# A gated activation that stays in its PSUM bank, its low part subtracted by VectorE instead of GpSimd

## The chip, the core and the metric

The kernel runs on one core of a Trainium2 chip. The core has five engines that run side by side and wait for each other through semaphores: TensorE (PE, matmuls; its weight loads are listed apart as PEld), VectorE (DVE), ScalarE (ACT), GpSimd (POOL) and SyncE (SP, which here only issues transfers). Data lies in SBUF and in PSUM, which has banks of 512 fp32 values per partition and takes the matmul results. The metric is the device time of one execution, in microseconds; lower is better.

## The reference

One decoder layer for 512 prompt tokens and 32 sample tokens: a mixer (RWKV-7 heads and windowed attention), and then PEER, a retrieval among 16384 experts. The change lies in PEER only, which is, cut down:

```python
def block(hb):                                  # hb: tokens x 1024
    q = (hb @ w_query).reshape(PEER_BLOCK, PEER_HEADS, 2, D_HALF)
    s = jnp.einsum('thcd,cnd->thcn', q, sub_keys)
    s1, i1 = lax.top_k(s[:, :, 0], PEER_TOPK)
    s2, i2 = lax.top_k(s[:, :, 1], PEER_TOPK)
    ...                                         # the best 16 of the sums, per head: idx, gate
    pre = jnp.einsum('td,tkd->tk', hb, eu[idx])
    act = jax.nn.gelu(pre, approximate=False) * gate
    return jnp.einsum('tk,tkd->td', act, ev[idx])
```

So every token picks 128 of the 16384 rows of `expert_u` and `expert_v` (eu, ev; 1024 values each).

## The kernel before

The prompt is cut into four tiles of 128 tokens. Two of them (tiles 0 and 3, and the 32 sample tokens) are done by **gathers**, the other two (1 and 2, together ND = 256 tokens) by the **dense part**, which multiplies by all 16384 experts, with gates that are zero where an expert was not picked.

*The gather side.* `experts` walks through a tile's 128 picks: GpSimd issues an indirect DMA that fetches one row of eu per token (`gat`, 128x1024, five buffers), VectorE makes a dot product of it into `pre`; after Gelu and gate, the same walk over ev, where VectorE adds `act * gat` to the sum (`x`). Each such gather with its use is a step of the queue `side`; `beside(n)` takes n steps on average.

*The dense part* runs over 128 blocks of 128 experts. All fp32 values are split into a high part (rounded to fp32r) and a low part (the rest), and products are made as high times high, low times high and high times low.
- `block_in` loads a block of eu and ev (`uv`), transposes eu through TensorE into two banks of the PSUM pool `w` (four banks in turn), copies the high part uH with ScalarE and takes the low part uL with VectorE; of ev, ScalarE makes vH and GpSimd makes vL.
- `block_u` multiplies with the tokens (24 matmuls into a bank `pre`, which the profile lists under `w`), takes Gelu in place on ScalarE, multiplies by the gates in two halves of 128 tokens on VectorE (the "gating": first half from `gl`, second from `gA` or `gB`), and splits the product into aH (ScalarE) and aL.
- `block_v` multiplies these with vH and vL into four banks `acc` (24 matmuls).

The loop calls `block_u(j+1)`, `block_in(j+2)`, `block_v(j)`, then up to two steps of `late`, which makes the projections and the top-k of tile 3 during the first blocks (the names that begin with l), and then three steps of the gather side:

```python
        for _ in range(LATE):
            next(more, None)
        with tc.issue_after(mark), tc.issue_after(sub):
            beside(RATE_D)
```

`mark` is the instruction that made aL, `sub` the last uL. The order on each engine is not the program's: the compiler's scheduler sets it when the kernel is built, from a model of its own, and `issue_after` only keeps the gather steps behind the instructions named, on the same engine.

Of the kernel before, what the change touches and what calls it, by code (L numbers as in the profile page):

```python
# [11 lines left out]
F32 = mybir.dt.float32  # L12
# [3 lines left out]
OP = mybir.AluOpType  # L16
# [97 lines left out]
def hymba_step(ctx, tc, x_prompt, x_sample, cache_k, cache_v, state_wkv, state_shift, meta, norm1_g, w_in, mu, w0,  # L114
# [3 lines left out]
    A, G, T, DM = nc.scalar, nc.gpsimd, nc.tensor, nc.sync  # L118
# [11 lines left out]
    V = V()  # L130
    uid = [0]

    def _t(pool, tag, bufs, shape, dt=F32):
        uid[0] += 1
        return pool.tile(list(shape), dt, tag=tag, name=f"{tag}_{uid[0]}", bufs=bufs)
# [1271 lines left out]
    ND = 256  # L1407
# [3 lines left out]
    def dt_(tag, bufs, shape, dt=F32):  # L1411
        return _t(dn, tag, bufs, shape, dt)

    def dps():
        return _t(dp, "w", 4, [128, 512])
# [40 lines left out]
    def block_u(x, g):  # L1456
        uH, uL, vH, vL = x
        pre = dps()[:, 0:ND]
        for k in range(8):
            T.matmul(pre, uH[:, k, :], hH[:, k, :], start=(k == 0), stop=False)  # L1460
            T.matmul(pre, uH[:, k, :], hL[:, k, :], start=False, stop=False)  # L1461
        for k in range(8):
            T.matmul(pre, uL[:, k, :], hH[:, k, :], start=False, stop=(k == 7))  # L1463
        ac = dt_("ac", 2, [128, ND])
        A.activation(pre, pre, AF.Gelu)  # L1465
        for i in range(2):
            V.tensor_tensor(ac[:, 128 * i:128 * i + 128], pre[:, 128 * i:128 * i + 128], g[i], OP.mult)
        aH = dt_("aH", 2, [128, ND], F32R)
        aL = dt_("aL", 2, [128, ND], F32R)
        A.copy(aH, ac)  # L1470
        return (vH, vL, aH, aL), G.tensor_tensor(aL, ac, aH.bitcast(F32), OP.subtract).ins  # L1471

    def block_v(j, x):
        vH, vL, aH, aL = x
# [98 lines left out]

    ins = {j: block_in(j)[0] for j in range(2)}
    mid, last = block_u(ins.pop(0), gate_of(0))
    for j in range(128):
        nxt, mark = None, last
        if j < 127:
            nxt, last = block_u(ins.pop(j + 1), gate_of(j + 1))
        if j < 126:  # L1580
            ins[j + 2], sub = block_in(j + 2)
        block_v(j, mid)
        mid = nxt
# [4 lines that stand above are left out]
# [45 lines left out]
```

## Time and profile before

| | us |
|---|---|
| median of 3 runs | 2225.62 |
| lowest and highest run | 2205.1 and 2230.73 |
| profiled execution | 2230.96 |
| its span in the trace | 2229.0 |
| busy in the span: TensorE, VectorE, GpSimd, ScalarE | 1852.5, 1712.3, 1426.3, 869.6 |

The profile is of one execution. Its busy times are shares of the whole span, which has a first part (mixer, up to about 1110 us), the making of the gate tables (to 1245 us), the dense part (to 2210 us) and an end of 19 us. Times of rows are microseconds from the start of the span. Line 126 is the helper through which every VectorE instruction is recorded, so VectorE's instructions are told apart by their tiles.

### The profile page before, as it was taken

How to read it: one execution, taken by the hardware profiler on the slowest of the kernel's cores; microseconds unless marked ns; L12 is line 12 of the kernel's file. 1: busy time of each engine (PE TensorE's matmuls, PEld its weight loads, DVE VectorE, ACT ScalarE, POOL GpSimd, SP SyncE). 2: the span in 40 equal slices, each digit the busy share in tenths (PEclk: the TensorE clock that was granted, in tenths of full speed). 3: DMA queues.
4: the chain of work that ended last, by engine and by line, in shares of the span. 5: the costliest groups of instructions: out<-in, count | busy, mean ns of one | idle time of the engine just before them, and what ended most of it. 6: DMA issues, size and time to landing. Idle time of an engine off the chain costs nothing.

```text
span 2229.0 us, 37454 instructions
## 1 busy us (share of the span) xinstructions
PE 1852.5 (83%) x13915; PEld 1720.4 (77%) x13915; DVE 1712.3 (77%) x3265; ACT 869.6 (39%) x1963; POOL 1426.3 (64%) x1091
## 2 busy tenths in 40 slices
PE   5899975585859858897366898899999999999995
PEld 5889974374737747786366888899999999999995
DVE  5543436788787888799889689987666688999897
ACT  6654421211313324223189534343444444343333
POOL 0110103878674767465615457899898999999996
PEclk9999996555655769998679999999999999999998
DMA  7532472687785798997667887799999999998886
GB/s 219 158 107 75 136 188 86 232 276 236 258 285 161 235 310 292 284 310 236 187 212 253 300 285 250 274 325 335 332 327 330 334 312 322 310 320 307 312 300 210
DMA packets 310156, 569.51 MB, mean 256 GB/s; under 512 B 32787, under 2 KB 194565, under 8 KB 309830
## 3 DMA queue, kind: packets, MB, share of 16 engines
q0 software_dynamic: 84048, 305.70, 39.7%
q1 hardware_dynamic: 225926, 261.43, 36.3%
q8 instruction: 109, 1.79, 0.3%
q14 instruction: 73, 0.60, 0.1%
HBM read 543.07 MB, written 24.60 MB: 255 GB/s over the span
## 4 chain that ended last, share of the span: by engine, by line
PE 38%; DVE 21%; issue 13%; POOL 12%; DMA 11%; ACT 4%; SPq 0%; DVEq 0%; POOLq 0%; ACTq 0%
POOL gat L1032 7%; DVE gat L126 4%; DVE x L126 4%; PE pD L218 3%; PE acc L1479 3%; PE acc L1480 3%; PE w L1463 3%; PE acc L1478 3%; PE w L1460 3%; PE w L1461 3%; DMA gat<-in_expert_u_dram,ei 2%; PE w L1446 2%; POOL aL L1471 2%; POOL vL L1453 2%; DMA gat<-in_expert_v_dram,ei 2%
## 5 line engine op out<-in xcount | busy, mean ns | idle before, releaser
L126 DVE SCALAR_TENSOR_TENSOR x<-gat,act,x 128x1024 f32<-128x1024 f32 x287 | 497.6, 1734 | 27.7 <-DMA gat<-in_expert_v_dram,ei 25.8
L1032 POOL DMA_INDIRECT gat<-in_expert_u_dram,ei x256 | 352.5, 1377 | 111.8 <-DVE pre L126 52.7
L1032 POOL DMA_INDIRECT gat<-in_expert_v_dram,ei x256 | 330.9, 1293 | 141.2 <-DVE x L126 41.3
L1453 POOL TENSOR_TENSOR vL<-uv,vH 128x1024 fp32r<-128x1024 f32 x128 | 314.8, 2460 | 20.7 <-ACT vH L1452 18.6
L1479 PE MATMUL acc<-aL,vH 128*128 128x256 f32 x1024 | 294.6, 289 | 20.1 <-POOL aL L1471 19.8
L1478 PE MATMUL acc<-aH,vH 128*128 128x256 f32 x1024 | 295.0, 296 | 4.0 <-ACT aH L1470 4.0
L1480 PE MATMUL acc<-aH,vL 128*128 128x256 f32 x1024 | 290.4, 285 | 0.0
L1460 PE MATMUL w<-dhH,uH 128*128 128x256 f32 x1024 | 253.7, 285 | 2.8 <-ACT lsc L1549 2.7
L1461 PE MATMUL w<-dhL,uH 128*128 128x256 f32 x1024 | 252.5, 284 | 0.0
L126 DVE CUSTOM_DVE_ANT_0 gat<-gat,h 128x1024 f32<-128x1024 f32 x160 | 213.1, 1341 | 47.3 <-DMA gat<-in_expert_u_dram,ei 45.0
L1452 ACT CAST vH<-uv 128x1024 fp32r<-128x1024 f32 x128 | 134.5, 1051 | 227.3 <-issue 121.9
L1479 PEld LDWEIGHTS acc<-aL,vH 128*128 128x128 f32 x1024 | 198.2, 194 | 26.6 <-POOL aL L1471 26.3
L126 DVE CUSTOM_DVE_ANT_0 gat<-gat,lx 128x1024 f32<-128x1024 f32 x128 | 199.7, 1583 | 8.7 <-DMA gat<-in_expert_u_dram,ei 8.6
L1460 PEld LDWEIGHTS w<-dhH,uH 128*128 128x128 f32 x1024 | 197.4, 193 | 3.5 <-ACT lsc L1549 3.1
L1478 PEld LDWEIGHTS acc<-aH,vH 128*128 128x128 f32 x1024 | 194.8, 194 | 4.5 <-ACT aH L1470 4.5
L1480 PEld LDWEIGHTS acc<-aH,vL 128*128 128x128 f32 x1024 | 198.2, 194 | 0.0
L1461 PEld LDWEIGHTS w<-dhL,uH 128*128 128x128 f32 x1024 | 197.3, 193 | 0.1
L126 DVE TENSOR_TENSOR uL<-w,uH 128x512 fp32r<-128x512 f32 x256 | 167.7, 683 | 11.4 <-ACT uH L1448 9.0
L1463 PE MATMUL w<-dhH,uL 128*128 128x256 f32 x1024 | 154.3, 290 | 12.7 <-DVE uL L126 12.4
L1471 POOL TENSOR_TENSOR aL<-ac,aH 128x256 fp32r<-128x256 f32 x128 | 137.9, 1077 | 29.5 <-ACT aH L1470 27.5
L126 DVE TENSOR_TENSOR ac<-w,gl 128x128 f32<-128x128 f32 x128 | 49.9, 390 | 137.3 <-ACT w L1465 120.1
L1448 ACT CAST uH<-w 128x512 fp32r<-128x512 f32 x256 | 139.5, 590 | 29.7 <-PE w L1446 19.2
(575 smaller groups left out, 4222.0 us busy)
## 6 DMA issues: line engine op xcount, KB each, us to landing
uv<-in_expert_u_dram SPq DMA_DIRECT2D x128, 512.0 KB, 4.6
uv<-in_expert_v_dram SPq DMA_DIRECT2D x128, 512.0 KB, 6.4
wst<-in_w_query_dram SPq DMA_DIRECT2D x48, 512.0 KB, 5.6
wst<-in_w_out_dram SPq DMA_DIRECT2D x24, 512.0 KB, 8.0
wst<-in_w_in_dram SPq DMA_DIRECT2D x20, 512.0 KB, 4.3
h2T<-in_w_in_dram SPq DMA_DIRECT2D x20, 512.0 KB, 4.1
gscr<-uv SPq DMA_DIRECT2D x10, 1024.0 KB, 6.2
gl<-gscr SPq DMA_DIRECT2D x16, 512.0 KB, 5.7
```

The source lines that it names most:

```text
L126: r = getattr(nc.vector, name)(*args, **kw)
L1032: G.indirect_dma_start(out=r, out_offset=None, in_=w[0], in_offset=bass.IndirectOffsetOnAxis(ap=ei[:, k:k + 1], axis=0))
L1448: A.copy(uH[:, ks, :], p)
L1452: A.copy(vH, vn)
L1453: G.tensor_tensor(vL, vn, vH.bitcast(F32), OP.subtract)
L1460: T.matmul(pre, uH[:, k, :], hH[:, k, :], start=(k == 0), stop=False)
L1461: T.matmul(pre, uH[:, k, :], hL[:, k, :], start=False, stop=False)
L1463: T.matmul(pre, uL[:, k, :], hH[:, k, :], start=False, stop=(k == 7))
L1471: return (vH, vL, aH, aL), G.tensor_tensor(aL, ac, aH.bitcast(F32), OP.subtract).ins
L1478: T.matmul(o, vH[:, ds_], aH, start=(j == 0 and d % 2 == 0), stop=False, skip_group_check=True)
L1479: T.matmul(o, vH[:, ds_], aL, start=False, stop=False, skip_group_check=True)
L1480: T.matmul(o, vL[:, ds_], aH, start=False, stop=(j == 127), skip_group_check=True)
```

## The change

The tile `ac` goes. The gating writes its product back into the bank `pre` that it read; ScalarE copies aH out of that bank; and the subtraction that makes aL moves from GpSimd to VectorE, which reads the bank and aH. GpSimd cannot be given it, as the operand is in PSUM. The instruction that `issue_after` names as `mark` is now one of VectorE.

```diff
-        ac = dt_("ac", 2, [128, ND])
         A.activation(pre, pre, AF.Gelu)
         for i in range(2):
-            V.tensor_tensor(ac[:, 128 * i:128 * i + 128], pre[:, 128 * i:128 * i + 128], g[i], OP.mult)
+            V.tensor_tensor(pre[:, 128 * i:128 * i + 128], pre[:, 128 * i:128 * i + 128], g[i], OP.mult)
         aH = dt_("aH", 2, [128, ND], F32R)
         aL = dt_("aL", 2, [128, ND], F32R)
-        A.copy(aH, ac)
-        return (vH, vL, aH, aL), G.tensor_tensor(aL, ac, aH.bitcast(F32), OP.subtract).ins
+        A.copy(aH, pre)
+        return (vH, vL, aH, aL), V.tensor_tensor(aL, pre, aH.bitcast(F32), OP.subtract).ins
```

Up to the second block of the dense part the order on every engine is as before; from there the scheduler gives another. GpSimd's queue at about block 105, while ev rows are gathered (`gat` is a gather), before:

```order
L1453 TENSOR_TENSOR vL_19685<-uv_19665,vH_19684 128x1024
L1032 DMA gat_17199<-in_expert_v_dram,ei_11_105 128x1024
L1032 DMA gat_17202<-in_expert_v_dram,ei_11_105 128x1024
L1471 TENSOR_TENSOR aL_19744<-ac_19739,aH_19743 128x256
L1453 TENSOR_TENSOR vL_19767<-uv_19747,vH_19766 128x1024
L1032 DMA gat_17285<-in_expert_v_dram,ei_11_105 128x1024
```

and after:

```order
L1453 TENSOR_TENSOR vL_19662<-uv_19642,vH_19661 128x1024
L1032 DMA gat_17300<-in_expert_v_dram,ei_11_105 128x1024
L1032 DMA gat_17303<-in_expert_v_dram,ei_11_105 128x1024
L1453 TENSOR_TENSOR vL_19741<-uv_19721,vH_19740 128x1024
L1032 DMA gat_17385<-in_expert_v_dram,ei_11_105 128x1024
L1032 DMA gat_17388<-in_expert_v_dram,ei_11_105 128x1024
```

Two gathers per block remain with vL; aL is gone. VectorE's queue at about block 109 (SCALAR_TENSOR_TENSOR is a gather add; a gating is `ac<-w,gl` or, after, `w<-w,gl`, and its second half has `gA`), before:

```order
L126 TENSOR_TENSOR ac_20139<-w_20114,gl_19712 128x128
L126 TENSOR_TENSOR ac_20139<-w_20114,gA_14431 128x128
L126 SCALAR_TENSOR_TENSOR x_3073_15057<-gat_17377,act_15054,x_3073_15057 128x1024
L126 TENSOR_TENSOR uL_20151<-w_20152,uH_20150 128x512
L126 TENSOR_TENSOR uL_20151<-w_20159,uH_20150 128x512
L126 SCALAR_TENSOR_TENSOR x_3073_15057<-gat_17380,act_15054,x_3073_15057 128x1024
```

and after:

```order
L126 TENSOR_TENSOR w_20005<-w_20005,gl_19608 128x128
L126 SCALAR_TENSOR_TENSOR x_3022_15006<-gat_17391,act_15003,x_3022_15006 128x1024
L126 TENSOR_TENSOR w_20005<-w_20005,gA_14387 128x128
L126 TENSOR_TENSOR uL_20041<-w_20042,uH_20040 128x512
L126 TENSOR_TENSOR uL_20041<-w_20049,uH_20040 128x512
L126 SCALAR_TENSOR_TENSOR x_3022_15006<-gat_17473,act_15003,x_3022_15006 128x1024
L126 TENSOR_TENSOR aL_20034<-w_20005,aH_20033 128x256
```

aL has come in, and in this block a gather add now stands between the two halves of the gating. VectorE's queue at the last two blocks, before:

```order
L126 SCALAR_TENSOR_TENSOR x_3073_15057<-gat_18535,act_15054,x_3073_15057 128x1024
L126 SCALAR_TENSOR_TENSOR x_3073_15057<-gat_18538,act_15054,x_3073_15057 128x1024
L126 SCALAR_TENSOR_TENSOR x_3073_15057<-gat_18541,act_15054,x_3073_15057 128x1024
L126 SCALAR_TENSOR_TENSOR x_3073_15057<-gat_18624,act_15054,x_3073_15057 128x1024
L126 TENSOR_TENSOR ac_21583<-w_21558,gl_20996 128x128
L126 TENSOR_TENSOR ac_21583<-w_21558,gA_14431 128x128
```

and after:

```order
L126 TENSOR_TENSOR aL_21381<-w_21352,aH_21380 128x256
L126 SCALAR_TENSOR_TENSOR x_3022_15006<-gat_18536,act_15003,x_3022_15006 128x1024
L126 SCALAR_TENSOR_TENSOR x_3022_15006<-gat_18539,act_15003,x_3022_15006 128x1024
L126 SCALAR_TENSOR_TENSOR x_3022_15006<-gat_18621,act_15003,x_3022_15006 128x1024
L126 TENSOR_TENSOR w_21431<-w_21431,gl_20876 128x128
L126 SCALAR_TENSOR_TENSOR x_3022_15006<-gat_18624,act_15003,x_3022_15006 128x1024
L126 TENSOR_TENSOR w_21431<-w_21431,gA_14387 128x128
L126 SCALAR_TENSOR_TENSOR x_3022_15006<-gat_18627,act_15003,x_3022_15006 128x1024
L126 TENSOR_TENSOR aL_21460<-w_21431,aH_21459 128x256
```

Three adds stand ahead of the last gating instead of four, and one each between its halves and ahead of aL.

## Rows read from the trace of the kernel before

**Rows 1.** Stretches: from:to, length, each engine's busy us (instructions), clock, DMA share, GB/s.

```profile
1310.00:1435.00 125.00, 106.56 (x849) 103.76 (x848) 122.78 (x340) 51.32 (x102) 93.21 (x79) 0.96 0.72 251
1435.00:1560.00 125.00, 119.31 (x991) 117.58 (x990) 100.46 (x143) 50.50 (x91) 115.41 (x75) 1.00 0.93 329
1560.00:1810.00 250.00, 250.00 (x2117) 250.00 (x2116) 170.25 (x298) 106.49 (x191) 227.34 (x150) 1.00 0.91 328
1810.00:2185.00 375.00, 361.10 (x2970) 354.76 (x2969) 336.57 (x326) 149.73 (x265) 351.20 (x218) 1.00 0.89 310
2185.00:2210.00 25.00, 18.61 (x133) 17.71 (x133) 18.83 (x16) 5.80 (x10) 22.04 (x18) 0.86 0.68 220
```

**Rows 2.** Waits of weight loads, 1810 to 2185: us in total, times, longest.

```profile
PEld acc L1479 <- POOL aL L1471: 15.5, 20, 2.6
PEld w L1463 <- DVE uL L126: 4.0, 8, 1.1
```

**Rows 3.** Waits of weight loads, 1310 to 1560.

```profile
PEld w L1463 <- DVE uL L126: 11.6, 6, 4.8
PEld acc L1479 <- POOL aL L1471: 6.2, 7, 1.9
PEld w L1446 <- DVE ac L126: 5.1, 2, 2.7
```

**Rows 4.** Groups of VectorE and GpSimd, 1810 to 2185: busy us, mean ns | idle before.

```profile
L126 DVE SCALAR_TENSOR_TENSOR x<-gat,act,x 128x1024 f32<-128x1024 f32 x112 | 246.2, 2198 | 4.1 <-DMA gat<-in_expert_v_dram,ei 3.1
L1453 POOL TENSOR_TENSOR vL<-uv,vH 128x1024 fp32r<-128x1024 f32 x54 | 132.4, 2452 | 0.9
L126 DVE TENSOR_TENSOR uL<-w,uH 128x512 fp32r<-128x512 f32 x108 | 71.0, 683 | 4.4 <-ACT uH L1448 4.0
L1471 POOL TENSOR_TENSOR aL<-ac,aH 128x256 fp32r<-128x256 f32 x53 | 62.0, 1171 | 0.9
L126 DVE TENSOR_TENSOR ac<-w,gB 128x128 f32<-128x128 f32 x23 | 6.5, 282 | 0.0
```

**Rows 5.** Timeline of one block: start, length, instruction, [idle before and releaser].

```profile
1995.89 0.39 DVE L126 TENSOR_TENSOR ac<-w,gl 128x128 f32<-128x128 f32 x1 [0.59 <-POOL aL L1471]
...
1996.20 0.40 DVE L126 TENSOR_TENSOR ac<-w,gA 128x128 f32<-128x128 f32 x1
...
1997.01 2.41 POOL L1453 TENSOR_TENSOR vL<-uv,vH 128x1024 fp32r<-128x1024 f32 x1
1997.74 4.10 DVE L126 SCALAR_TENSOR_TENSOR x<-gat,act,x 128x1024 f32<-128x1024 f32 x2
...
2001.35 1.07 POOL L1471 TENSOR_TENSOR aL<-ac,aH 128x256 fp32r<-128x256 f32 x1
...
2002.51 0.39 DVE L126 TENSOR_TENSOR ac<-w,gl 128x128 f32<-128x128 f32 x1 [0.68 <-POOL aL L1471]
```

**Rows 6.** Timeline at 1365 us, and the group of first gatings, 1310 to 1435.

```profile
1365.72 0.73 POOL L1471 TENSOR_TENSOR aL<-ac,aH 128x256 fp32r<-128x256 f32 x1
...
1365.92 1.61 DVE L126 CUSTOM_DVE_ANT_0 gat<-gat,lx 128x1024 f32<-128x1024 f32 x1
...
1367.76 1.20 DVE L126 CUSTOM_DVE_ANT_0 gat<-gat,lx 128x1024 f32<-128x1024 f32 x1
...
L126 DVE TENSOR_TENSOR ac<-w,gl 128x128 f32<-128x128 f32 x11 | 4.1, 373 | 0.0
```

**Rows 7.** Timeline of the last block.

```profile
2198.19 3.66 DVE L126 SCALAR_TENSOR_TENSOR x<-gat,act,x 128x1024 f32<-128x1024 f32 x1 [1.53 <-DMA gat<-in_expert_v_dram,ei]
...
2202.51 0.41 ACT L1470 CAST aH<-ac 128x256 fp32r<-128x256 f32 x1 [5.58 <-DVE ac L126]
...
2205.76 0.74 POOL L1471 TENSOR_TENSOR aL<-ac,aH 128x256 fp32r<-128x256 f32 x1
...
2206.55 0.58 PE L1479 MATMUL acc<-aL,vH 128*128 128x256 f32 x1 [2.38 <-POOL aL L1471]
...
2210.49 1.91 PE L1600 MATMUL w<-ident,gB 128*128 128x128 f32 x16
```

## The prediction

> **What bounds the kernel now.** I read the stretches first, because the dense part (1245 to 2210 us) has several regimes. A row of [rows 1] gives, for one stretch, each engine's busy time, how many matmuls ran, and the clock granted to TensorE. From 1560 to 1810 TensorE is busy 250.00 of 250 us: 2117 matmuls, or 8.47 per us. A block has 24 matmuls against h, 8 transposes and 24 matmuls into the accumulators, 56 in all, so it takes 6.61 us there, and nothing but fewer matmuls could shorten that stretch. Measured against that rate the other stretches show what is lost, and the count sees more than the busy time, which leaves out the refilling of the pipeline after a wait:
> - 1310 to 1435: 849 matmuls where 1058 would fit, 24.7 us short (some belong to the late tile's projections and are slower, so this is an upper bound). VectorE is busy 122.78 of 125 us: it is the bound.
> - 1435 to 1560: 991, 8.0 us short.
> - 1810 to 2185: 2970 where 3175 would fit, 24.3 us short. GpSimd is busy 351.20 of 375 us (94%), VectorE 336.57 (90%).
> - 2185 to 2210: 133 where 212 would fit, 9.3 us short, with the clock granted at 0.86.
>
> Next come TensorE's waits in those stretches. From 1810 to 2185 weight loads wait 15.5 us for aL of GpSimd, against 4.0 us for uL of VectorE [rows 2]. So of the 24.3 us lost, 15.5 / 19.5, or 19.3 us, hang on aL. From 1310 to 1560 VectorE is named first: 11.6 us for uL and 5.1 us for ac, with 6.2 us for aL [rows 3].
>
> Why aL is late in the third stretch is seen in the groups [rows 4]. GpSimd has vL (2452 ns), aL (1171 ns) and two gathers in every 6.62 us, the distance of two gatings in [rows 5] (1995.89 and 2002.51). aL stands in its queue behind a gather and, in [rows 5], starts at 2001.35, 5 us after its gating. A gather add takes 2198 ns in the mean here. The two adds of [rows 5] last 4.10 us beside a vL of 2.41 us, while a dot product over the same 128x1024 elements took 1.20 us with no GpSimd subtraction beside it [rows 6]. VectorE and GpSimd hold each other up.
>
> **The change part by part.** *GpSimd loses 128 subtractions.* They took 1171 ns each in the third stretch; 53 of them there are 62.0 us [rows 4], so GpSimd falls from 351 to about 289 us of 375 and stops being the bound. The 19.3 us of waits for it go.
>
> *VectorE gains 128 subtractions.* No row shows a 128x256 one. Between the 128x128 gating, 282 ns, and the 128x512 uL, 683 ns [rows 4], a line through both gives 282 + 401/3 = 416 ns; I take 0.42, with the two rows as ends. The operand kinds are those of uL (one input in PSUM, one in SBUF, output fp32r in SBUF). In the third stretch 53 x 0.42 is 22 us.
>
> *The gating writes PSUM.* No row shows VectorE writing PSUM. The second gating now writes the tile that the first one wrote and waits for it, where before it began 0.31 us after a start of 0.39 us length (1995.89 and 1996.20 in [rows 5]). I price that at 0.1 us each, 13 us of VectorE in all; the ends are 0 and the 0.39 us of a whole gating. ScalarE's copy aH, 0.41 us from SBUF [rows 7], now reads PSUM. ScalarE was busy 149.73 of 375 us [rows 1], so I price the difference at nothing; if that idle time were gone, it could be no more than the 0.41 us again.
>
> *VectorE's order.* In the built order the second gating has a gather add ahead of it in 46 of the 128 blocks (4 before), and aL has at least one add between the first gating and itself in 96. Who waits for that: ScalarE's aH behind the second gating, then aL, then TensorE's v matmuls. The deadline is generous: v of block j follows u and the transposes of the next blocks, 6.62 + 8/8.47 = 7.6 us after u of block j ended. For a block whose order is gating, add, gating, uL, uL, add, aL, with adds as short as the free dot product (1.20 us [rows 6]) and 0.4 us for Gelu ahead, taken like aH, which has as many values, I get 0.4 + 0.4 + 1.2 + 0.4 + 1.4 + 1.2 + 0.4 = 5.4 us; with adds of 2.2 us it is 7.4 us. So some blocks will wait. As bounds: nothing, or half a microsecond (the mean of the eight uL waits, 4.0 / 8 [rows 2]) in each of the 46 blocks, 23 us. I take 8 us, nearer to the row for uL, since VectorE's products now come late twice as often.
>
> *The same pool turn is held longer.* The bank of `pre` is free only after aL instead of after the gating. Transposes take it two blocks on, at the deadline just named less 0.9 us; where aL meets its own deadline by a microsecond this costs nothing, and otherwise it is within the 23 us.
>
> *The late top-k, 1310 to 1435.* VectorE is the bound, so its additions count in full. The stretch has 11 gatings [rows 6], hence 11 x 0.52 = 5.7 us. The new order also pulls four gather steps forward (23 instead of 19 in blocks 9 to 16), 4 x 1.20 = 4.8 us. Against it stands relief: a dot product that began beside aL lasted 1.61 us, the next without it 1.20 [rows 6], so 0.41 us for the aL of each of the 11 blocks, 4.5 us. Net 6.0 us later; the ends are 0 (relief as large as the cost) and 10.5 (none). The 6.2 us of waits for aL in 1310 to 1560 I leave unspent, since VectorE, which is late there anyway, now makes aL.
>
> What the row shows of the mutual holding, 4.10 us for two adds beside one vL [rows 5], is what the Trainium skill, "SBUF — State Buffer", section "Who interferes with whom", states as a rule: an instruction of VectorE with two SBUF inputs and one of GpSimd that reads SBUF exclude each other for the whole instruction, and one with a single SBUF input takes no part. By that rule the new aL excludes nobody, and the old one's whole time comes back to VectorE; that is the first rival. The row agrees for vL; no row shows a VectorE subtraction with a PSUM input running free beside GpSimd for its whole length.
>
> *The end.* The last block's gating stands behind a gather add of 3.66 us, so that ScalarE waits 5.58 us and begins aH at 2202.51; aL begins at 2205.76 on GpSimd, behind three gathers in the order; TensorE waits 2.38 us for it, and the output transposes begin at 2210.49 [rows 7]. Now three adds stand ahead of that block's gating instead of four, and five gather steps come after its start instead of eight; gating, add, gating, add, aL is 0.4 + 1.2 + 0.4 + 1.2 + 0.4 = 3.6 us, about what passed from aH to aL before (3.25). So what comes forward is the start, by one add, 1.2 us if free and 3.7 if held like the last one; I take 3, nearer to that row.
>
> The sum against the profiled execution (2230.96 us): -19.3 + 8 + 6.0 - 3 = -8.3, or 2222.7. That execution lies 0.24% above the median of the runs, 2225.62, so on the median's scale the forecast is **2217 us**, 0.4% less. The part before 1245 us keeps its order and adds nothing.
>
> **The rivals.** *First, the holding eases more than the order costs.* GpSimd's readers of SBUF in the third stretch are vL (132.4 us) and aL (62.0): a third of the time that an add can be held goes. Adds are 2198 ns against 1.2 for the free dot product, two per block, so 0.6 us per block would come back, more than the 0.52 added. Then VectorE is no slower anywhere: the late stretch gains its aL share (6.2 of 22.9 us of waits [rows 3], or 8.9 of the 24.7 + 8.0 us lost), the new waits fall to none, half of the rest in the third stretch (24.3 less 19.3) goes as well, and -19.3 - 8.9 - 2.5 - 3 = -33.7, or 2192 on the median's scale. The rule of the Trainium skill, "SBUF — State Buffer", section "Who interferes with whom", would make this case the likeliest. For it: the 1.61 against 1.20. Against it: in 1560 to 1810 nothing can be gained, and the late stretch is VectorE's own.
>
> *Second, slower: aL and the gating are stuck behind gather adds.* The mechanism is the order above, in the 46 blocks; it decides once the mean add stays above 2.2 us, where the chain reaches 7.4 of its 7.6 us. The adds measure 2198 ns now, so it is close. The price is 23 us of new waits, and 10.5 in the late stretch, with nothing won at the end: -19.3 + 23 + 10.5 = +14, or 2240. It would show first as idle TensorE in 1560 to 1810, where there is none now. Against it: vL holds at most one of a block's two adds.
>
> *Third, the wait only changes its name.* TensorE waits as long for VectorE's aL as for GpSimd's: -19.3 + 19.3 + 6.0 - 3 = +3, or 2229.
>
> **How the numbers follow.** A measurement of this kernel can tell about 1% from no change: 2203 to 2248 is the same. Forecast 0.46, first rival 0.28, second 0.17, third 0.09. The forecast's own ends, with new waits of 3 and 13 us, a late stretch of 3 and 10.5 and an end of 3.7 and 1.2, are 2209 and 2228. The range reaches to the first two rivals, 2192 to 2240. Faster by over 1%: most of the first rival and a little of the forecast, 0.30; slower by over 1%: half of the second, 0.08; within 1%, 0.62.
>
> **What would show it.** Right: no wait of TensorE for GpSimd's aL; GpSimd under 80% busy from 1810 on; that stretch at over 8.2 matmuls per us; aL near 0.42 us on VectorE; a longer late stretch. The first rival shows in adds under 1.8 us in the mean; the second in waits for aL on VectorE from 1560 to 1810; the third in waits for it equal to the old ones. I would be wrong altogether if VectorE's writes to PSUM cost much more than 0.39 us, or if the reordered start of the side work shifted the DMA load.

## The result, and the profile after

| | before | after |
|---|---|---|
| median of the runs | 2227.64 us (2205.1 to 2230.73, 4 runs) | 2194.48 us (2185.03 to 2204.76, 4 runs) |
| profiled execution, its span | 2230.96, 2229.0 us | 2204.76, 2203.0 us |
| ratio of the medians | | 0.9849, 95% interval 0.9811 to 0.9887 |

The change makes the kernel 1.5% faster. The same kernel run again gave 2194.4 us, where the kernel before had a median of 2223.92 over 20 runs: 0.9843 [0.9802, 0.9883]. The forecast was 2217; the first rival's time was 2192. Both profiled executions of the changed kernel (2204.76 and 2207.67) are the slowest of their runs, and that of before is slower than each of its runs; the two traces are 26 us apart where the medians are 33 (29.5 in the second comparison).

The stretches of the dense part after (from:to, length, busy us and instructions of PE, PEld, DVE, ACT, POOL, clock, DMA share, GB/s):

```profile
1310.00:1435.00 125.00, 103.39 (x809) 100.48 (x807) 120.83 (x348) 50.31 (x100) 85.46 (x72) 0.95 0.77 263
1435.00:1560.00 125.00, 121.67 (x1007) 120.69 (x1008) 100.26 (x167) 51.22 (x91) 85.13 (x57) 0.99 0.93 344
1560.00:1810.00 250.00, 250.00 (x2118) 250.00 (x2117) 199.23 (x336) 105.23 (x191) 184.53 (x114) 1.00 0.90 325
1810.00:2160.00 350.00, 348.10 (x2932) 347.90 (x2931) 283.96 (x371) 145.93 (x261) 250.74 (x162) 1.00 0.92 331
2160.00:2185.00 25.00, 21.95 (x170) 21.54 (x170) 20.69 (x23) 8.52 (x16) 17.95 (x12) 0.93 0.60 196
```

Against [rows 1]: from 1810 on TensorE does 2932 matmuls in 350 us, 8.38 per us, where it did 2970 in 375, 7.92 per us. At 8.47 per us 2963 would fit, so 3.7 us are lost there instead of 24.3 (the window ends 25 us earlier because the last blocks come earlier). GpSimd is down from 94% to 72%. VectorE, which took over 53 subtractions in that stretch, is not fuller: 284 of 350 us, 81%, where it was 90%. From 1310 to 1435 fewer matmuls ran than before (809 against 849), from 1435 to 1560 some more (1007 against 991).

The waits of weight loads after, first those from 1310 to 1560 (answering to [rows 3]), then the only one from 1810 to 2160 (answering to [rows 2]):

```profile
PEld acc L1478 <- DVE aL L126: 15.2, 7, 4.6
PEld w L1544 <- DVE uL L126: 5.0, 2, 4.2
PEld w L1463 <- DVE uL L126: 3.7, 4, 1.7
...
PEld acc L1478 <- DVE aL L126: 2.1, 1, 2.1
```

Twenty waits for aL have become one in the third stretch. In the late top-k the wait for aL has grown from 6.2 to 15.2 us and changed its engine, while uL fell from 11.6 to 3.7 (and 5.0 of the late tile's own).

The groups from 1810 to 2160 (busy us, mean ns | idle time before and what ended it), as in [rows 4]:

```profile
L126 DVE SCALAR_TENSOR_TENSOR x<-gat,act,x 128x1024 f32<-128x1024 f32 x110 | 176.0, 1600 | 0.4
L1453 POOL TENSOR_TENSOR vL<-uv,vH 128x1024 fp32r<-128x1024 f32 x53 | 131.4, 2480 | 25.2 <-ACT vH L1452 24.6
...
L126 DVE TENSOR_TENSOR aL<-w,aH 128x256 fp32r<-128x256 f32 x53 | 22.1, 417 | 5.3 <-ACT aH L1469 5.3
L126 DVE TENSOR_TENSOR w<-w,gl 128x128 f32<-128x128 f32 x52 | 20.6, 396 | 58.9 <-ACT w L1464 58.9
L1469 ACT CAST aH<-w 128x256 fp32r<-128x256 f32 x52 | 19.8, 382 | 24.4 <-DVE w L126 24.2
```

This is where the time came from. A gather add takes 1600 ns in the mean instead of 2198. With two adds per block VectorE gets 2 x 0.598 = 1.2 us per block back and pays 0.417 us for aL, so it gains although it was given work.

The single adds show what lengthened them. An add that is not held takes 1.26 to 1.34 us. From 1810 us to the end of the span, 50 of the 125 adds before began while a subtraction of GpSimd was running (more than 0.1 us before its end), and every one of them ended 1.08 to 1.17 us after that subtraction did; after the change 14 of 120 began so, and ended 1.08 to 1.09 us after it. In the windows of the two tables (to 2185 and to 2160) 77 of 112 adds were longer than 1.35 us before, and 19 of 110 after. Of the 103 us that those 77 took beyond the free length, 86 fell to adds that met vL alone, 8 to adds that met aL alone, and 9 to adds that met both; after, vL's share is 36. So about three quarters of what VectorE got back are not aL's own holding: with aL gone, far fewer adds are held by vL (52 before, 19 after). The idle time of GpSimd ahead of vL, 0.9 us in [rows 4] and 25.2 us here, nearly all of it waiting for vH, fits that: vL no longer stands behind other work, and starts as soon as ScalarE has made vH. That this is why it meets fewer adds was not tried by itself.

One block in the timeline of VectorE, then of GpSimd (start, length, instruction, count; answering to [rows 5]):

```profile
1992.09 0.40 DVE L126 TENSOR_TENSOR w<-w,gl 128x128 f32<-128x128 f32 x1 [1.75 <-ACT w L1464]
1992.52 0.42 DVE L126 TENSOR_TENSOR w<-w,gA 128x128 f32<-128x128 f32 x1
1992.85 1.28 DVE L126 TENSOR_TENSOR uL<-w,uH 128x512 fp32r<-128x512 f32 x2
1994.05 0.41 DVE L126 TENSOR_TENSOR aL<-w,aH 128x256 fp32r<-128x256 f32 x1
1994.38 2.60 DVE L126 SCALAR_TENSOR_TENSOR x<-gat,act,x 128x1024 f32<-128x1024 f32 x2
...
1991.15 2.41 POOL L1453 TENSOR_TENSOR vL<-uv,vH 128x1024 fp32r<-128x1024 f32 x1
1993.72 0.95 POOL L1032 DMA_INDIRECT gat<-in_expert_v_dram,ei  x1 [0.16 <-DVE uL L126]
1995.93 1.86 POOL L1032 DMA_INDIRECT gat<-in_expert_v_dram,ei  x1 [1.26 <-DVE x L126]
```

vL runs from 1991.15 to 1993.56. Beside it VectorE does both gatings and part of a pair of uL at their usual lengths; each of these reads one operand from PSUM. The two adds, which read SBUF twice, come after vL has ended and take 2.60 us together, against 4.10 us for the pair beside vL in [rows 5].

The last block (answering to [rows 7]), from VectorE, then ScalarE and TensorE:

```profile
2175.75 3.10 DVE L126 SCALAR_TENSOR_TENSOR x<-gat,act,x 128x1024 f32<-128x1024 f32 x1
2178.77 0.37 DVE L126 TENSOR_TENSOR w<-w,gA 128x128 f32<-128x128 f32 x1
2179.05 1.27 DVE L126 SCALAR_TENSOR_TENSOR x<-gat,act,x 128x1024 f32<-128x1024 f32 x1
2180.25 0.41 DVE L126 TENSOR_TENSOR aL<-w,aH 128x256 fp32r<-128x256 f32 x1
...
2179.23 0.37 ACT L1469 CAST aH<-w 128x256 fp32r<-128x256 f32 x1 [4.77 <-DVE w L126]
...
2180.72 0.39 PE L1478 MATMUL acc<-aL,vH 128*128 128x256 f32 x1 [0.32 <-DVE aL L126]
```

From aH to aL's start it is now 1.02 us (3.25 before), but a held add of 3.10 us still stands between the two halves of the gating, so that aH waits 4.77 us.

Where the time went is told by the starts of the Gelu of the same block in both traces. Block 0 starts 1.2 us earlier (1245.15, 1243.99), the last block of the middle stretch, 72, 0.8 earlier (1807.33, 1806.53), block 127 22.5 earlier (2196.57, 2174.09); from there to the output transposes it is 10.30 us instead of 13.92 (2210.49 less 2196.57). So blocks 0 to 72 lose 0.4 us, blocks 72 to 127 gain 21.7, the end gains 3.6, and 1.2 come from ahead of the dense part: 26.1 of 26.2 us. Those 1.2 us can't be put down to the change. That the order on every engine is as before up to the second block does not hold for GpSimd: the load of h (at 1307.21 us before, at 1172.88 after) and two gathers now come ahead of the first vL instead of behind it. But in the ten traces of this case the Gelu of block 0 starts anywhere from 1235.95 to 1246.55 us, with either order.

### The profile page after: what moved, and what is told of

It is laid out like the page before. It is cut to its first block, busy times and chain, and to the rows that moved or that the text cites. A ratio compares the mean times of both kernels' runs of the same rounds, so it can differ in the third digit from the quotient of the medians.

```text
span 2203.0 us, 37197 instructions
## 1 busy us (share of the span) xinstructions
PE 1839.1 (83%) x13915; PEld 1716.0 (78%) x13915; DVE 1690.4 (77%) x3393; ACT 867.3 (39%) x1963; POOL 1249.2 (57%) x963
## 4 chain that ended last, share of the span: by engine, by line
PE 51%; DVE 22%; DMA 10%; issue 9%; POOL 5%; ACT 3%; SPq 0%; DVEq 0%; POOLq 0%; ACTq 0%
DVE gat L126 5%; PE acc L1478 5%; PE w L1460 5%; PE w L1461 5%; PE w L1463 5%; PE acc L1479 5%; PE acc L1477 5%; PE w L1446 4%; POOL gat L1032 4%; DVE x L126 4%; PE pD L218 3%; DMA gat<-in_expert_v_dram,ei 3%; PE ps L218 2%; DMA wst<-in_w_query_dram 2%; DMA gat<-in_expert_u_dram,ei 2%
## 5 line engine op out<-in xcount | busy, mean ns | idle before, releaser
L126 DVE SCALAR_TENSOR_TENSOR x<-gat,act,x 128x1024 f32<-128x1024 f32 x287 | 427.9, 1491 | 24.7 <-DMA gat<-in_expert_v_dram,ei 23.4
L1032 POOL DMA_INDIRECT gat<-in_expert_u_dram,ei x256 | 343.0, 1340 | 158.8 <-DVE pre L126 75.7
L1032 POOL DMA_INDIRECT gat<-in_expert_v_dram,ei x256 | 294.4, 1150 | 193.6 <-DVE x L126 73.1
L1453 POOL TENSOR_TENSOR vL<-uv,vH 128x1024 fp32r<-128x1024 f32 x128 | 322.5, 2519 | 56.1 <-ACT vH L1452 54.3
L1477 PE MATMUL acc<-aH,vH 128*128 128x256 f32 x1024 | 280.5, 295 | 5.3 <-ACT aH L1469 5.3
L1478 PEld LDWEIGHTS acc<-aL,vH 128*128 128x128 f32 x1024 | 200.6, 196 | 19.3 <-DVE aL L126 19.3
L126 DVE CUSTOM_DVE_ANT_0 gat<-gat,lx 128x1024 f32<-128x1024 f32 x128 | 214.4, 1686 | 0.0
L1477 PEld LDWEIGHTS acc<-aH,vH 128*128 128x128 f32 x1024 | 188.0, 193 | 6.0 <-ACT aH L1469 5.9
L126 DVE TENSOR_TENSOR w<-w,gl 128x128 f32<-128x128 f32 x128 | 50.5, 395 | 143.3 <-ACT w L1464 143.2
L1446 PE MATMUL w<-ident,uv 128*128 128x128 f32 x1024 | 141.4, 273 | 0.0
```

Of the source, the lines that this page charges most:

```text
L126: r = getattr(nc.vector, name)(*args, **kw)
L1032: G.indirect_dma_start(out=r, out_offset=None, in_=w[0], in_offset=bass.IndirectOffsetOnAxis(ap=ei[:, k:k + 1], axis=0))
L1446: T.transpose(p[:, q, :], un[:, 128 * k:128 * k + 128], ident)
L1453: G.tensor_tensor(vL, vn, vH.bitcast(F32), OP.subtract)
L1477: T.matmul(o, vH[:, ds_], aH, start=(j == 0 and d % 2 == 0), stop=False, skip_group_check=True)
L1478: T.matmul(o, vH[:, ds_], aL, start=False, stop=False, skip_group_check=True)
```

## The experiments

Two theories stood against each other. *Holding*: GpSimd's aL kept VectorE's gather adds off SBUF (and they it), and with it gone VectorE and GpSimd both have room. *Queue*: aL was late only because it stood behind vL and gathers in GpSimd's queue; VectorE's shorter adds are a by-product. A third, *order*, was that the gain comes from where the scheduler puts the gather adds. Two further questions were what the PSUM operand is worth, and in which blocks the gain and the cost lie. Each ratio is to runs of the kernel before taken beside that kernel, 19 with a median of 2227.18 us or the 20 with 2223.92; the median is given with it.

**The subtraction on VectorE, from SBUF.** The kernel before, with one letter changed; `ac` stays.

```diff
-        return (vH, vL, aH, aL), G.tensor_tensor(aL, ac, aH.bitcast(F32), OP.subtract).ins
+        return (vH, vL, aH, aL), V.tensor_tensor(aL, ac, aH.bitcast(F32), OP.subtract).ins
```

> The gated product goes to SBUF (ac) as before, and VectorE, not GpSimd, subtracts from there: two SBUF inputs. Queue theory (GpSimd was too full from 1810 us on, and aL stood in its queue): the gain is that of the change, a ratio to the kernel before of 0.983 to 0.989, since GpSimd's queue is as empty. Holding theory (the gain is that VectorE and GpSimd no longer hold each other at the low part, for which an operand in PSUM is needed): the subtraction is held beside vL, its mean rises from 0.415 us to over 0.6 us, and at least a third of the gain is gone, ratio above 0.990. Order theory (the gain comes from where the scheduler puts the gather adds): the order differs from both kernels, so anything from 0.985 to 1.0 with waits for aL on VectorE.

Measured: 2200.02 us, 0.9869 [0.982, 0.9917], against 2227.18. Two of its groups from 1810 to 2160, and then one aL of VectorE's timeline and the vL beside it:

```profile
L126 DVE SCALAR_TENSOR_TENSOR x<-gat,act,x 128x1024 f32<-128x1024 f32 x108 | 178.6, 1654 | 0.4
...
L126 DVE TENSOR_TENSOR aL<-ac,aH 128x256 fp32r<-128x256 f32 x52 | 32.6, 626 | 0.0
...
2003.13 2.79 DVE L126 TENSOR_TENSOR aL<-ac,aH 128x256 fp32r<-128x256 f32 x1
...
2003.24 2.38 POOL L1453 TENSOR_TENSOR vL<-uv,vH 128x1024 fp32r<-128x1024 f32 x1
```

An aL of the changed kernel that lies inside a vL, for comparison, in its timeline:

```profile
2022.99 0.41 DVE L126 TENSOR_TENSOR aL<-w,aH 128x256 fp32r<-128x256 f32 x1
...
2022.96 2.39 POOL L1453 TENSOR_TENSOR vL<-uv,vH 128x1024 fp32r<-128x1024 f32 x1 [0.51 <-ACT vH L1452]
```

With both operands in SBUF the subtraction takes 626 ns in the mean instead of 417; the adds are nearly as short as after the change. The mean is made of two kinds: an aL that meets no vL takes about 0.41 us in nearly all cases, and the one shown is held for the whole of its vL (2.38 + 0.41 = 2.79). Over the whole trace 15 of the 128 overlap a vL. Five of these take 0.40 to 0.42 us, since they began first or almost with it; where the one of 2153.08 and its vL began within 0.2 us of each other, it is vL that lasts 2.85 us. The other ten take 1.1 to 2.8 us. In the changed kernel 35 overlap a vL, 14 of them lying wholly inside one, and the longest of the 35 takes 0.43 us. The kernel's time lies within the noise of the change's. So the gain is the move of the subtraction off GpSimd; what the bank as an operand adds, 0.2 us of VectorE per block, can't be told from nothing in the total. Of the expectations, the time is the one that the queue theory gave, 0.983 to 0.989; the holding theory had the subtraction right (over 0.6 us beside vL) but the total wrong (above 0.990), for only 15 of the 128 meet a vL. The order theory is weakened: only 5 second gatings have a gather step ahead of them here, against 46 in the changed kernel, and the gain is there all the same.

**An idle subtraction on GpSimd.** The changed kernel, with a subtraction of the old shape put back on GpSimd. Nothing reads its result, and the old tile name `ac` serves for it.

```diff
         A.copy(aH, pre)
+        idle = dt_("ac", 2, [128, ND])
+        G.tensor_tensor(idle, aH.bitcast(F32), aH.bitcast(F32), OP.subtract)
```

> The change, and besides it GpSimd still makes a subtraction of the old size per block, of aH from itself, which nobody reads: work added, results unchanged. Queue theory in its narrow form (only the place of aL in the queue mattered): GpSimd is over 90% busy from 1810 us on again, TensorE does not wait, and the ratio stays at 0.983 to 0.990. Queue theory in its wide form (a full GpSimd also delays vL and the gathers): TensorE waits for vL, or VectorE for gathers, ratio 0.992 to 1.000. Holding theory: the adds rise to 2.1 us again from about 1.6, VectorE has 0.5 us per block more than it can do, and TensorE waits for uL and aL of VectorE: ratio 0.995 to 1.010.

Measured: 2227.8 us, 1.0014 [0.9978, 1.0051], against 2227.18. Two stretches, two groups and the waits from 1810 on:

```profile
1560.00:1810.00 250.00, 246.34 (x2064) 244.23 (x2063) 233.94 (x329) 103.00 (x184) 230.54 (x148) 1.00 0.90 319
1810.00:2160.00 350.00, 338.05 (x2804) 332.74 (x2802) 335.66 (x353) 139.13 (x251) 322.09 (x204) 1.00 0.90 315
...
L126 DVE SCALAR_TENSOR_TENSOR x<-gat,act,x 128x1024 f32<-128x1024 f32 x104 | 235.1, 2261 | 1.9 <-DMA gat<-in_expert_v_dram,ei 1.6
...
L1471 POOL TENSOR_TENSOR ac<-aH 128x256 f32<-128x256 f32 x49 | 54.9, 1121 | 2.4 <-ACT aH L1469 1.6
...
PEld w L1463 <- DVE uL L126: 11.7, 17, 1.2
PEld acc L1480 <- DVE aL L126: 3.8, 5, 2.5
```

TensorE needs nothing of what was put back, and yet the whole gain is gone: the adds are at 2261 ns, VectorE is at 96% from 1810 on, and TensorE waits for uL and aL of VectorE. That is what the second rival described, and even the stretch from 1560 to 1810, in which TensorE never idled, loses matmuls (2064 against 2118). VectorE's adds waited only 1.6 us for gathers, and TensorE not at all for vL. But this edit also fills GpSimd's queue, so the queue theory isn't out by it: what stands behind the idle subtraction can come later.

**Same queue place, with and without reads of SBUF.** Two kernels that settle this. Both put one unread instruction per block straight behind vL in GpSimd's queue; the order on all engines is otherwise identical in the two, but for two instructions of the late top-k on VectorE. One zeroes 128x768 elements and reads nothing; the other subtracts 256 columns of vH from themselves and reads SBUF twice. `low` keeps vL's instruction.

```diff
+        with tc.issue_after(low[id(vL)]):
+            idle = dt_("ac", 1, [128, 768])
+            G.memset(idle, 0.0)
```

> The change, and besides it GpSimd sets a tile of 128x768 to zero in each block, right behind vL: work added, results unchanged. It fills GpSimd's queue but reads nothing. Length unknown, between 0.4 and 1.2 us. If the idle subtraction of the earlier run took the gain away by filling the queue, this takes at least half of it too (ratio 0.992 or above) where it lasts 0.7 us or more. If it did so by reading SBUF beside VectorE, the gather adds stay near 1.6 us and the ratio at 0.983 to 0.990.

```diff
+        with tc.issue_after(low[id(vL)]):
+            idle = dt_("ac", 2, [128, ND])
+            hi = vH[:, 0:ND].bitcast(F32)
+            G.tensor_tensor(idle, hi, hi, OP.subtract)
```

> The twin of the run with the idle zeroing: at the same place in GpSimd's queue, behind vL, a subtraction of 128x256 of vH from itself, two reads of SBUF, 0.72 us when free. The order on VectorE and GpSimd is the same in both. Holding theory: gather adds above 2.0 us from 1810 us on and a ratio of 0.995 to 1.008. Queue theory: the same ratio as its twin, within 0.005, for the same time on GpSimd.

Measured, against 2223.92: 2201.95 us, 0.9898 [0.9866, 0.993] for the zeroing; 2233.23 us, 1.0027 [0.9997, 1.0057] for the reading one. The stretch and two groups of the zeroing kernel:

```profile
1810.00:2160.00 350.00, 344.55 (x2885) 343.93 (x2884) 288.45 (x366) 143.82 (x258) 290.70 (x213) 0.99 0.92 325
...
L126 DVE SCALAR_TENSOR_TENSOR x<-gat,act,x 128x1024 f32<-128x1024 f32 x107 | 181.2, 1693 | 0.3
...
L1474 POOL MEMSET ac<- 128x768 f32 x52 | 38.7, 745 | 0.0
```

The same of the reading kernel, its two largest waits of weight loads in that stretch, and one add of its timeline with GpSimd's instructions beside it:

```profile
1810.00:2160.00 350.00, 337.76 (x2813) 334.52 (x2812) 318.40 (x352) 139.81 (x249) 325.23 (x205) 1.00 0.90 315
...
L126 DVE SCALAR_TENSOR_TENSOR x<-gat,act,x 128x1024 f32<-128x1024 f32 x104 | 218.1, 2097 | 14.1 <-DMA gat<-in_expert_v_dram,ei 13.8
...
L1475 POOL TENSOR_TENSOR ac<-vH 128x256 f32<-128x256 f32 x51 | 76.2, 1494 | 0.0
...
PEld acc L1484 <- DVE aL L126: 7.6, 7, 1.3
PEld w L1465 <- DVE uL L126: 5.0, 3, 2.5
...
1989.96 3.49 DVE L126 SCALAR_TENSOR_TENSOR x<-gat,act,x 128x1024 f32<-128x1024 f32 x1
...
1989.97 2.39 POOL L1455 TENSOR_TENSOR vL<-uv,vH 128x1024 fp32r<-128x1024 f32 x1
1992.31 1.61 POOL L1475 TENSOR_TENSOR ac<-vH 128x256 f32<-128x256 f32 x1
```

The shortest of the reading subtractions took 602 ns, less than the zeroing's 745; in the mean it took 1494. The add at 1989.96 lasts 3.49 us: vL's 2.39 and then its own 1.1. The subtraction behind vL then takes 1.61 us, most of it until the add has ended (1993.45). So at the same place in the queue the reader costs all of the gain, 31 us more than the zeroing. From the Gelu of block 72 to that of block 127 the reading kernel takes 390.2 us, as the kernel before (389.2); the zeroing one takes 373.4, the changed kernel 367.6 and 366.1 in its two traces.

How the reads cost that much is not split further. The adds are longer (2097 ns), but the held subtractions also lengthen GpSimd's queue (325 us busy of 350 against 291), and VectorE's adds wait 13.8 us for gathers, where the zeroing has 0.3 us of idle time there in all. Both follow from the holding. The zeroing itself took away about a third of the gain (1.0% is left of 1.5%), which seven and six runs can only just tell from nothing; so GpSimd's time alone may be worth something, but it is the smaller part. Holding stands; the queue theory as the main cause falls.

**In which blocks.** Three kernels make the change only for some of the blocks (`j` is the block's number); the others keep `ac` and GpSimd.

```diff
+        moved = j >= 72
+        ac = pre if moved else dt_("ac", 2, [128, ND])
...
+        return (vH, vL, aH, aL), (V if moved else G).tensor_tensor(aL, ac, aH.bitcast(F32), OP.subtract).ins
```

With `j >= 72`, the third stretch and the end only:

> The change from block 72 on only, about where the gathers turn from eu to ev rows and GpSimd was fullest; blocks 0 to 71 as before. Queue and holding theories: nearly the whole gain, ratio 0.984 to 0.990. If the first 72 blocks carried it, or the new order as a whole, 0.995 or above.

With `j < 72`:

> The change in blocks 0 to 71 only; from block 72 as before. Queue and holding theories: no gain, ratio 0.997 to 1.003, with TensorE waiting 10 to 20 us for aL of GpSimd after 1810 us. Order theory: some of the gain, 0.990 or below.

With `j >= 16`, so that the late top-k keeps the old order:

> The change from block 16 on; the first 16 blocks, in which VectorE is the bound because of the late top-k, leave ac in SBUF and aL to GpSimd. If the change costs what the prediction put on that stretch (6 us), this is 0.2 to 0.3% faster than the changed kernel; if relief and cost cancel there, the two are equal within 0.002.

Measured: from 72 on, 2205.18 us, 0.9886 [0.9846, 0.9925]; up to 71, 2221.04 us, 0.9988 [0.9957, 1.0018], both against 2227.18; from 16 on, 2193.94 us, 0.9851 [0.9816, 0.9885], against 2223.92. Up to 71, the third stretch is as it was before the change (the first wait and the adds from 1810 to 2160):

```profile
PEld acc L1480 <- POOL aL L1472: 15.2, 22, 1.8
...
L126 DVE SCALAR_TENSOR_TENSOR x<-gat,act,x 128x1024 f32<-128x1024 f32 x105 | 226.7, 2159 | 6.9 <-DMA gat<-in_expert_v_dram,ei 6.1
```

So most of the gain lies in blocks 72 to 127 and the end (1.1% of the 1.5%, and the rest is within the noise), and the first 72 blocks give nothing that can be measured by themselves. Whether it helps to spare the late top-k, the times can't tell: 2193.94 against 2194.4 us for the changed kernel, whose six runs spread over 24 us. The trace of the kernel from 16 on does show a difference. From the Gelu of block 0 to that of block 72 it takes 555.5 us, where the two traces with the old order there (before, and from 72 on) took 562.2 and 564.6 and the changed kernel 562.5 and 563.9; from 1435 to 1560 it loses nothing:

```profile
1435.00:1560.00 125.00, 125.00 (x1058) 124.93 (x1057) 98.19 (x171) 52.13 (x95) 93.37 (x58) 1.00 0.93 348
```

**The changed kernel again**, beside the twins.

> The changed kernel itself, for a comparison on one chip with the run from block 16 on: 0.982 to 0.988 of the kernel before.

Measured: 2194.4 us, 0.9843 [0.9802, 0.9883], against 2223.92. Its trace has the same third stretch as the first one of the change: nothing is lost up to 2150, with 2879 matmuls in 340 us (2878 in the first trace), or 8.47 per us, and the one wait for aL, 2.1 us, comes behind that in both:

```profile
1810.00:2150.00 340.00, 340.00 (x2879) 340.00 (x2878) 273.67 (x361) 143.41 (x258) 245.99 (x159) 1.00 0.92 334
```

Between blocks 0 and 72 it loses 1.7 us against before (Gelu of block 0 at 1246.55, of block 72 at 1810.4, where before had 1245.15 and 1807.33), between 72 and 127 it gains 23.2, and at the end 2.5 (11.43 us from the last Gelu to the output transposes).

## Why the prediction was right in its direction and short in its size

The direction, the stretch, and the wait that goes were right. The forecast's 8.3 us became 26 between the traces. That 2194 lies inside the stated range, 2192 to 2240, is owed to the first rival, to which the range had been stretched; the forecast by itself reached down to 2209, and faster by over 1% had been given a chance of 0.30. By its own steps:

- *The 19.3 us of waits for aL go.* Right, and a little more: blocks 72 to 127 gained 21.7 us (23.2 in the second trace), as the waits for uL went too.
- *New waits, 8 us.* **This is the step that failed.** From 1560 to 1810 there are none, from 1810 to 2160 one of 2.1 us, and the same in the second trace. The order is as feared (a gather add ahead of the second gating in 46 blocks), but the wait was priced with adds that stay long. The step weighed a chain of 5.4 us with free adds against 7.4 us with adds of 2.2, then took its price from the waits for uL in the trace before, where the adds were held by aL. The change that put aL behind the adds also shortened them to 1600 ns, most of all because fewer of them meet vL. With the adds at 2261 and 2097 ns again, in the two kernels with a reading idle subtraction, the feared waits for uL and aL came (15.5 and 12.6 us from 1810 to 2160). So the second rival's point of decision, 2.2 us, was of about the right size, and the changed kernel was just never near it.
- *The late top-k, +6.0 us.* The cost came, nearly at its price; what was missing is a gain behind it. From the Gelu of block 0 to that of block 24 (at about 1486 us) before takes 240.6 us, the two traces of the change 244.6 and 245.9: 4.0 and 5.3 us lost. The relief that was set against the cost did not come there: a dot product from 1310 to 1435 takes 1805 ns in the mean, 1628 before. From block 24 to block 36 both take 79.55 us instead of 83.25, and 3.7 us come back: the waits for aL (2.2 us) and uL (1.1 us) that before had there are gone. The prediction left this unspent. So 0.4 or 1.7 us remain over blocks 0 to 72. The kernel with the change from block 16 on fits: 238.0 us to block 24, and 79.0 from there to 36. One reading of the rows was wrong here: the late tile's matmuls from 1310 to 1435 (L1545 before) are not slower than the others, with 112 ns from start to start in a run of them against 109 to 120.
- *The prices of the single instructions.* aL 0.417 us (0.42 taken). The first half of the gating 396 ns in PSUM, where [rows 5] has 0.39; the second 404 and 295 ns for its two operands, where before had 390 and 282. The second half does wait for the first, as was feared: where the two stand next to each other it starts 0.43 us after it in the median of 66 pairs, 0.31 before, so the 0.1 us was well priced. ScalarE's copy took 382 ns, where [rows 7] has 0.41 us from SBUF. All about as priced, or less.
- *The end, -3.* Right: -3.6, and -2.5 in the second trace. The start came earlier by no whole add, though: 4.77 us of waiting for 5.58. Most of it is the shorter way from aH to aL, 1.02 us for 3.25, which I had taken as equal.

The sum with the measured terms: -21.7 + 0.4 - 3.6 - 1.2 (ahead of the dense part) = -26.1. The medians' 33 us contain 7 more, which no trace here shows; the traces are of the slower executions, and the start of the dense part alone differs by up to 10 us between traces.

The first rival is what happened in its mechanism: the holding eases by more than the order costs. It put the time that comes back at 0.6 us per block, as aL's share of GpSimd's reading time; the adds gave 1.2, of which aL takes 0.42 again. The surplus is that vL, too, holds fewer of them, which the rival did not foresee. Its third stretch and end, -19.3 - 2.5 - 3 = -24.8, stand against -25.3 measured; its late stretch, -8.9, did not come, so that its 2192 fits the median better than it fits the traces. The Trainium skill, "SBUF — State Buffer", section "Who interferes with whom", has the rule behind it, and the prediction said that by this rule the rival would be the likeliest. The trace agrees on each side that was open: an aL with one SBUF input ran at 0.41 us inside a vL, and of 35 that overlap one none was longer than 0.43; the same aL with two SBUF inputs took up to 2.8; and the zeroing, which reads no SBUF, left the adds at 1693 ns where the reading subtraction took them to 2097. I had held against it that nothing could be gained where TensorE was full, which was true and didn't matter: the gain was needed only where the adds were long.

The third rival, the wait that only changes its name, is seen in one place: from 1310 to 1560, where 6.2 us for GpSimd's aL became 15.2 for VectorE's. It cost little there, since the waits for uL and `ac` fell as that for aL rose: 22.9 us for the three before, 23.9 after with the late tile's uL, and 28.5 and 28.3 for all waits of weight loads in that stretch.

## What to carry to other kernels

Before you price a move from GpSimd to VectorE as so many microseconds more on VectorE, look at how long VectorE's two-input instructions are with and without GpSimd beside them: where the mean is well above the free length, removing GpSimd's instruction may give back more than it costs. Count, add by add, which instruction of GpSimd each one met: the one that you remove need not be the one that held most. Price each term at the lengths that the change leaves, not at those of the trace before: a wait that depends on a length that the change alters belongs in one sum with it. To learn whether an engine's instruction costs by its place in the queue or by what it reads, replace it by one that reads nothing and has the same place.

## What was not expected of the hardware

- The holding is mutual, and each instruction waits for the rest of the other: an add, which is 1.26 to 1.34 us long where nothing holds it, took 3.49 us beside a vL of 2.39, and the 128x256 subtraction behind it, 602 ns at its shortest, took 1.61.
- An unread 128x256 subtraction on GpSimd cost the whole kernel 31 us more than an unread zeroing of three times the elements at the same place.
- A gather's issue on GpSimd took 0.95 us in one place of a block and 1.86 in another (1993.72 and 1995.93 above). The traces show it waiting for adds in the same way. From 1810 to 2180, the 40 issues before and the 74 after that began beside no running add took 0.93 to 0.99 us. Of the others, 68 of 69 before and 29 of 42 after ended 0.81 to 0.83 us after the add that was running; the rest had begun together with the add and took 0.93 to 0.95. No run was made to test it by itself.
- A single gating was no dearer with its output in PSUM than in SBUF beyond 5 to 14 ns; what the shared bank cost is the 0.12 us by which the second half starts later behind the first.
